# Quarter sums of w_down: made within the MLP's down product instead of beside the cross-attention

## The chip, the cores and the metric

The kernel runs on one core of one Trainium2 chip. The metric is the device time of one execution in microseconds, the median of the runs; lower is better. A profile is one further execution, taken with the hardware profiler.

## The reference

One inference step of a small streaming encoder: two layers over 1024 prompt frames and 64 sample frames (1088 columns), model width 1024, all in fp32. What matters here is the second half of every layer, and w_down above all:

```python
def cross_attn(h, mk, mv, w_q, w_o):
    q = (h @ w_q).reshape(B, L, N_MEM_HEADS, MEM_HEAD_DIM)
    s = jnp.einsum('blhd,bmhd->bhlm', q, mk).astype(jnp.float32) * (MEM_HEAD_DIM ** -0.5)
    pr = jax.nn.softmax(s, axis=-1)
    o = jnp.einsum('bhlm,bmhd->blhd', pr.astype(mv.dtype), mv).reshape(B, L, D_MODEL)
    return o @ w_o
def sq_relu_mlp(h, w_up, w_down):
    return jnp.square(jax.nn.relu(h @ w_up)) @ w_down
...
        x = x + cross_attn(rmsnorm(x, ...), mem_k[layer], mem_v[layer], p['w_mq'][layer], p['w_mo'][layer])
        x = x + sq_relu_mlp(rmsnorm(x, ...), p['w_up'][layer], p['w_down'][layer])
```

w_up is 1024 x 4096 and w_down 4096 x 1024. There are four attention heads of width 256 and 256 memory tokens.

## The kernel before, in words

**Split products.** fp32 operands go to TensorE as two fp32r parts. A split is an ACT copy that makes the high part and a DVE subtraction that makes the low part (`split`, L238 and L241; for whole weight tiles `Weights.do_split`, L185 and L186). A product takes three matmuls: low x high, high x low, high x high.

**Stages.** A memory stage and the mixer of layer 0 come first. Then each layer has its cross-attention (`cross`, for columns s = 0 of width 512 and s = 1 of width 576, each followed by `project_back` with w_mo), the up product and the down product of the MLP; layer 1 has a window attention ahead of its cross-attention.

**Cross-attention.** For each head j, `query(j)` makes two blocks of queries from w_mq tiles (`mm<-hpH,wp`), DVE scales them (L824), ACT and DVE split them into qh and ql; `scores(j)` multiplies them with k and does the softmax; `flip(j-1)` transposes the probabilities of the head before and splits them (tp); `values(j-1)` multiplies them with v. Work of one head thus stands between the steps of the next.

**Up and down products.** Both use a seven-product scheme on 2 x 2 blocks. In the down product, w_down is cut into eight groups g of 512 rows; a group has four quarters [128 x 2 x 512] (column half c, row tiles r and r + 2). `SEVEN` lists seven products m. Three of them take a quarter as it lies in w_down: (0,0), (1,1), (0,1). Four take a sum: S1 = q(1,0) + q(1,1), S3 = q(0,0) - q(1,0), S2 = S1 - q(0,0), S4 = q(0,1) - S2. The order is (0,0), (1,1), S3, S1, S2, S4, (0,1), so the products are called m0 to m6 here.

**Where the sums are made.** Before, `weights_sums` makes all four sums for a whole layer while its cross-attention runs: 32 pieces, each fetched by two DMAs that ACT issues (L966), combined by four POOL operations of 128 x 256 (L960) and stored to a scratch tensor `sums` by a DMA that ACT issues (L969). `cross` advances this generator with `next(beside)` at eight places per head. ACT works its queue in order, so a store that waits for POOL holds up what stands behind it.

**The down product's steps.** `mlp_down` has 14 steps, two halves of each m, four groups each. A step multiplies four weight tiles with four u tiles for both s. For every group of the next step it calls `W.ahead` (split a staged weight, load a later one) and `load_u` (fetch a u tile `ur` of 544 KB and split it into `uhl`). Weights land in three staging buffers `st` (`Weights.load`, L173): a load can start when the split of the weight three before it is done. Split tiles have five buffers `wd` and three `wp`, one for each group; u tiles have three buffers `ur`. All these loads stand in SP's queue. The Tile scheduler decides the order on each queue; the up product alone has a manual order on SP, POOL and PE.

```python
    for i, (m, half) in enumerate(steps):          # mlp_down
        ...
                    if after is not None and s == 0:
                        W.ahead(c + 1)
                        g = 4 * after[1] + c
                        ready[after[0], g] = load_u(us, p, after[0], g)
```

Of the kernel before, what the change touches and what calls it, by code (L numbers as in the profile page):

```python
# [7 lines left out]
F32 = mybir.dt.float32  # L8
# [5 lines left out]
D = 1024  # L14
KC = D // 128
NT1 = 512
NT2 = 576
# [16 lines left out]
S2, S3, S4, S1 = range(4)  # L34
# [12 lines left out]
def body(ctx, tc, I, O):  # L47
# [4 lines left out]
    def dram(t, offset, ap):  # L52
        return bass.AP(tensor=t.tensor, offset=t.offset + offset, ap=ap)
# [65 lines left out]
    def plan_mlp(l):  # L119
        stops.append(len(plan))  # L120
        w = I["w_down"][l]
        for m, (q, *_) in enumerate(SEVEN):
            for g in range(8):
                if isinstance(q, int):
                    src = sums[l][g][:, q]
                else:
                    src = dram(w, (4 * g + q[1]) * 128 * D + q[0] * 512, [[D, 128], [256 * D, 2], [1, 512]])
                plan.append((("down", l, m, g), "s", [(slice(0, 128), None, src)]))

    stops = []  # L130
    sums = [[scr.tile([128, 4, 2, 512], F32, name=f"sums{l}_{g}") for g in range(8)] for l in range(2)]
# [16 lines left out]
    class Weights:  # L148
        def __init__(self):
            self.loaded, self.split, self.used = 0, 0, 0  # L150
            self.stage, self.tiles = {}, {}
            self.staged, self.more = 0, None
            self.stop, self.room = stops[0], 3

        def load(self):

            if self.loaded >= self.stop or self.staged >= self.room:
                return False
            key, kind, pieces = plan[self.loaded]
            self.staged += 1  # L160
            st = wst.tile([128, 1024], F32, tag="st", name="st")
            for rows, part, src in pieces:
                if kind == "n":
                    dst = st.rearrange("p (k n) -> p k n", n=128)
                elif kind == "d":
                    dst = st.rearrange("p (k n) -> p k n", n=256)
                elif kind == "s":
                    dst = st.rearrange("p (k n) -> p k n", n=512)
                elif kind == "q":
                    dst = st.rearrange("p (k h n) -> p k h n", h=2, n=64)[:, :, part]  # L170
                else:
                    dst = st.rearrange("p (q k n) -> p q k n", q=2, n=128)[rows, part]
                nc.sync.dma_start(dst, src)  # L173
            self.stage[self.loaded] = st
            self.loaded += 1
            return True

        def do_split(self):
            st = self.stage.pop(self.split)
            key, kind, pieces = plan[self.split]  # L180
# [600 lines left out]
    def cross(l, s, norm, p, then, beside):  # L781
# [25 lines left out]
        def query(j):  # L807
# [3 lines left out]
            for c in range(2):  # L811
# [9 lines left out]
                next(beside)  # L821
# [14 lines left out]
        def scores(j):  # L836
            qh, ql = st["q", j]
            ps_of = []
            for q, bl in groups:
# [21 lines left out]
                if len(ps_of) == 1:  # L861
                    next(beside)
# [57 lines left out]
        for j in range(4):  # L920
            q = query(j)
            next(q)
            next(beside)
# [3 lines left out]
            next(beside)  # L927
            next(q, None)
            next(beside)
# [4 lines left out]
            next(beside)  # L934
            scores(j)
            load_kv(j + 1, 0, 1)
            next(beside)
# [6 lines left out]

    def weights_sums(l, p):


        keep = tc.keep_in_program_order
        tiles = {}

        def at(i):
            return sums[l][i // 4][:, :, i // 2 % 2, 256 * (i % 2):256 * (i % 2) + 256]

        for i in range(34):
            if 1 <= i <= 32:

                a = tiles[i - 1]
                for to, one, two, op in ((3, 1, 3, OP.add), (1, 0, 1, OP.subtract), (0, 3, 0, OP.subtract),
                                         (2, 2, 0, OP.subtract)):
                    keep(pool.tensor_tensor(a[:, to], a[:, one], a[:, two], op))  # L960
            if i < 32:
                a = tiles[i] = p.tile([128, 4, 256], F32, tag="quarters", name="quarters", bufs=2)
                for j in range(2):
                    rows = I["w_down"][l][256 * (i // 2) + 128 * j:256 * (i // 2) + 128 * j + 128]
                    rows = rows.rearrange("p (h n) -> p h n", h=2)[:, :, 256 * (i % 2):256 * (i % 2) + 256]
                    keep(act.dma_start(a[:, 2 * j:2 * j + 2], rows))  # L966
            yield
            if 1 <= i <= 32:
                keep(act.dma_start(at(i - 1), tiles.pop(i - 1)))  # L969
            yield  # L970
# [280 lines left out]
    def mlp_down(l, us, ready, last, p):  # L1251
# [19 lines left out]
        for i, (m, half) in enumerate(steps):  # L1271
# [4 lines left out]
            for s in range(2):  # L1276
# [4 lines left out]
                for c in range(4):  # L1281
# [369 lines left out]
    def main():  # L1651
# [36 lines left out]
        for l in range(2):  # L1688
# [12 lines left out]
            with phase(f"cross{l}") as p:  # L1701
                nexts = []
                beside = weights_sums(l, p)
                back = cross(l, 0, c1, p, lambda: nexts.append(prepared(1, G_CROSS + l)), beside)
                project_back(**back)
                back = cross(l, 1, nexts[0], p, lambda: nexts.append(prepared(0, G_MLP + l, True)), beside)
                for _ in beside:
                    pass
# [50 lines left out]
```

## Time and profile before

| | us |
|---|---|
| median of 3 runs | 2867.02 (2865.0 to 2870.07) |
| profiled execution, its own time | 2863.92 |
| its span | 2862.1 |
| PE busy | 2688.7 (94%) |
| DVE / ACT / POOL busy | 1661.9 / 1240.1 / 788.3 |
| granted TensorE clock over the span, share of full | 0.974 |
| DMA traffic | 414.22 MB, 145 GB/s mean |

Between the span and the execution's own time lie 1.8 us. PE is the busiest engine, but its share is a mean over stages: it is near 100% in the up and down products and near 80% in parts of the cross-attention. A profile of this kind is read by stage: first which stretch has idle time on PE, then what ended that idle time, then what the releasing engine had itself waited for.

### The profile page before, as it was taken

The numbers are of one execution on the slowest core, as the hardware profiler recorded it, in microseconds if no ns is written. First come the engines' busy times: TensorE is split into PE (matmuls) and PEld (weight loads), VectorE is DVE, ScalarE is ACT, GpSimd is POOL, SyncE is SP. The second block draws the span as 40 slices with busy tenths as digits, with TensorE's granted clock in tenths as the row PEclk, the third lists the DMA queues.
The fourth block names the chain that finished last, engine by engine and source line by source line (L and its number), as shares of the span: only waits on it lengthen the run. The fifth ranks groups of instructions, "written<-read, shape, count | busy, mean of one in ns | idle before, by whom it ended". The sixth has DMA issues, their size and how long they took to land. (4 is left out here: it accounts for less than half of the span.)

```text
span 2862.1 us, 47830 instructions
## 1 busy us (share of the span) xinstructions
PE 2688.7 (94%) x19048; PEld 2550.2 (89%) x19048; DVE 1661.9 (58%) x2834; ACT 1240.1 (43%) x2099; POOL 788.3 (28%) x878
## 2 busy tenths in 40 slices
PE   8999997979899999999999999879898999999998
PEld 8978996778799999999988899768798999999998
DVE  5596754556855456555457467455577454555453
ACT  5584542434444345333337347243444344443334
POOL 3200025343455652000003013343524655500000
PEclk9999998999999999999999999999999999999999
DMA  8722246564244447555331321556623444575552
GB/s 266 227 74 81 67 129 200 151 212 142 63 138 151 134 140 270 191 183 182 99 88 29 87 68 45 166 175 191 203 69 118 135 129 154 167 244 181 181 182 78
DMA packets 442276, 414.22 MB, mean 145 GB/s; under 512 B 50001, under 2 KB 398177, under 8 KB 442053
## 3 DMA queue, kind: packets, MB, share of 16 engines
q1 hardware_dynamic: 364548, 316.99, 35.5%
q10 hardware_dynamic: 68608, 67.12, 7.2%
q0 software_dynamic: 8896, 27.06, 3.0%
q8 instruction: 149, 2.44, 0.4%
q14 instruction: 75, 0.61, 0.1%
HBM read 301.84 MB, written 109.39 MB: 144 GB/s over the span
## 5 line engine op out<-in xcount | busy, mean ns | idle before, releaser
L219 PE MATMUL mm<-hpH,wp 128*128 128x288 f32 (+3 forms) x3008 | 725.5, 329 | 4.8 <-DVE wp L186 2.6
L219 PEld LDWEIGHTS mm<-hpH,wp 128*128 128x128 f32 x3008 | 517.1, 190 | 44.2 <-DVE wp L186 3.2
L219 PE MATMUL mm<-hpL,wp 128*128 128x288 f32 (+3 forms) x1504 | 473.6, 330 | 2.2 <-DVE hpL L299 2.2
L185 ACT ACTIVATE wp<-st 128x1024 fp32r<-128x1024 f32 x218 | 229.4, 1057 | 332.0 <-PE mm L219 207.9
L241 DVE TENSOR_TENSOR wp<-st,wp 128x512 fp32r<-128x512 f32 x238 | 197.7, 838 | 240.3 <-ACT wp L238 238.1
L219 PE MATMUL s<-T,wp 128*128 128x256 f32 (+1 forms) x2304 | 310.3, 292 | 24.5 <-DVE wp L241 11.5
L186 DVE TENSOR_TENSOR wp<-st,wp 128x1024 fp32r<-128x1024 f32 x218 | 270.9, 1244 | 95.5 <-ACT wp L185 94.0
L219 PEld LDWEIGHTS s<-T,wp 128*128 128x128 f32 x2304 | 299.5, 191 | 30.0 <-DVE wp L241 14.9
L219 PEld LDWEIGHTS mm<-hpL,wp 128*128 128x128 f32 x1504 | 287.8, 191 | 22.1 <-DVE hpL L299 3.3
L960 POOL TENSOR_TENSOR quarters<-quarters 128x256 f32<-128x256 f32 x256 | 220.1, 862 | 277.3 <-DMA quarters<-in_w_down_dram 259.3
L324 POOL TENSOR_TENSOR rc<-rc,mhalf 128x4 f32<-128x4 f32 (+1 forms) x21 | 22.6, 1084 | 892.5 <-DVE rc L323 892.5
L238 ACT ACTIVATE wp<-st 128x512 fp32r<-128x512 f32 x238 | 136.2, 620 | 227.8 <-POOL st L1083 203.9
L219 PE MATMUL mm<-B,wp 128*128 128x256 f32 (+1 forms) x1536 | 204.8, 289 | 0.0
L185 ACT ACTIVATE wd<-st 128x1024 fp32r<-128x1024 f32 x70 | 73.6, 1054 | 301.7 <-PE t L1292 291.0
L219 PEld LDWEIGHTS mm<-B,wp 128*128 128x128 f32 x1536 | 197.7, 189 | 0.0
L186 DVE TENSOR_TENSOR wd<-st,wd 128x1024 fp32r<-128x1024 f32 x70 | 85.6, 1225 | 151.5 <-ACT wd L185 151.5
L1290 PE MATMUL s<-uhl,wd 128*128 128x256 f32 x560 | 156.4, 281 | 3.2 <-DVE uC L1113 1.8
L1291 PE MATMUL s<-uhl,wd 128*128 128x256 f32 x560 | 157.2, 281 | 0.8 <-DVE uhl L241 0.8
L241 DVE TENSOR_TENSOR uhl<-ur,uhl 128x1088 fp32r<-128x1088 f32 x112 | 144.7, 1295 | 22.6 <-ACT uhl L238 22.5
L1292 PE MATMUL s<-uhl,wd 128*128 128x256 f32 x560 | 156.6, 280 | 0.0
L238 ACT ACTIVATE uhl<-ur 128x1088 fp32r<-128x1088 f32 x112 | 123.4, 1104 | 54.7 <-DMA ur<-u 51.8
L1135 POOL TENSOR_TENSOR ss<-uC 128x288 f32<-128x288 f32 (+1 forms) x64 | 55.3, 864 | 327.7 <-ACT uC L1134 268.5
(402 smaller groups left out, 6336.1 us busy)
## 6 DMA issues: line engine op xcount, KB each, us to landing
ur<-u SPq DMA_DIRECT2D x112, 544.0 KB, 6.1
st<-in_w_up_dram SPq DMA_DIRECT2D x68, 512.0 KB, 5.0
quarters<-in_w_down_dram ACTq DMA_DIRECT2D x128, 256.0 KB, 3.7
sums<-quarters ACTq DMA_DIRECT2D x64, 512.0 KB, 4.1
st<-sums SPq DMA_DIRECT2D x64, 512.0 KB, 5.8
st<-in_w_down_dram SPq DMA_DIRECT2D x48, 512.0 KB, 5.2
st<-in_w_mq_dram SPq DMA_DIRECT2D x32, 512.0 KB, 4.3
st<-in_w_mo_dram SPq DMA_DIRECT2D x32, 512.0 KB, 4.3
```

The lines of the kernel that those rows point to most:

```text
L185: act.activation(wt[:, 0], st, AF.Copy)
L186: dve.tensor_tensor(wt[:, 1], st, f32(wt[:, 0]), OP.subtract)
L219: m = pe.matmul(ps, a, b, start=i == 0, stop=i == len(terms) - 1)
L238: act.activation(h, src, AF.Copy)
L241: dve.tensor_tensor(l, src, f32(h), OP.subtract)
L324: pool.tensor_tensor(rc[:m, b0:b1], rc[:m, b0:b1], mhalf[:m, b0:b1], OP.pow)
L960: keep(pool.tensor_tensor(a[:, to], a[:, one], a[:, two], op))
L1135: pool.tensor_tensor(t[0], u[:, 3], u[:, 0], OP.subtract)
L1290: pe.matmul(ps, wl, uh, start=first, stop=False)
L1291: pe.matmul(ps, wh, ul, start=False, stop=False)
L1292: pe.matmul(ps, wh, uh, start=False, stop=half == 1 and g == 3 and k == 1)
```

## The change

`weights_sums` and all `next(beside)` are taken out of `cross`. The sums are made in the down product, when a weight is loaded: `Weights.load` fetches one quarter (or a kept sum) into `st`, the new `combine` fetches the other operand in two DMAs of 256 KB into a pair of small buffers, and POOL adds or subtracts in place in `st`, two operations of 128 x 512 for each operand. Three pairs of small buffers take turns: `sx` in the down phase's own pool, and the norm's `rb` and `ss`/`sq`. S1 of the even groups is made during m1 and kept in `sums`; S1 of the odd groups during m3; S2 of the even groups is kept during m4. Stores of kept sums are issued by POOL. The calls of `W.ahead` and `load_u` move from the four c of s = 0 to every second c of both s.

Counted for a layer: 36 operands fetched (72 DMAs of 256 KB), 72 POOL operations of 128 x 512, 12 kept sums of 512 KB stored, in place of 128 POOL operations of 128 x 256, 64 fetches of 256 KB and 32 stores of 512 KB. Loads and stores in a step, u tiles among them and two small fetches taken as one: 8 in m0 and m6, on average 12 in m1, m2 and m3, 14 in m4 and m5.

```diff
-                if isinstance(q, int):
-                    src = sums[l][g][:, q]
+                s1, s2, odd = sums[l][g][:, 0], sums[l][g][:, 1], g % 2
+                if q == S3:
+                    src, more, keep = quarter(0, 0), [(OP.subtract, quarter(1, 0))], None
+                elif q == S1:
+                    src, more, keep = (quarter(1, 0), [(OP.add, quarter(1, 1))], s1) if odd else (s1, [], None)
+                elif q == S2:
+                    src, more, keep = s1, [(OP.subtract, quarter(0, 0))], None if odd else s2
+                elif q == S4:
+                    src, keep = quarter(0, 1), None
+                    more = [(OP.add, quarter(0, 0)), (OP.subtract, s1)] if odd else [(OP.subtract, s2)]
                 else:
...
+                    if q == (1, 1) and not odd:
+                        more, keep = [(None, quarter(1, 0))], s1
...
+        def combine(self, st, more, keep):
+
+            for op, src in more:
+
+                tag = ("sx", "rb", "ss")[self.turn % 3]
+                self.turn += 1
+                both = []
+                for i in range(2):
...
+                    both.append(t[:, :512])
+                    nc.sync.dma_start(both[i], src[:, i])
+                for i, t in enumerate(both):
+                    part = st[:, 512 * i:512 * i + 512]
+                    if op is None:
+                        pool.tensor_tensor(t, part, t, OP.add)
+                        pool.dma_start(keep[:, i], t)
+                    else:
+                        pool.tensor_tensor(part, part, t, op)
+            if more and more[0][0] is not None and keep is not None:
+                pool.dma_start(keep, st.rearrange("p (k n) -> p k n", n=512))
...
-    def weights_sums(l, p):
...
-                    if after is not None and s == 0:
-                        W.ahead(c + 1)
-                        g = 4 * after[1] + c
+                    if after is not None and c % 2 == 0:
+                        W.ahead(2 * s + c // 2 + 1)
+                        g = 4 * after[1] + 2 * s + c // 2
                         ready[after[0], g] = load_u(us, p, after[0], g)
```

**ACT's queue in the cross-attention.** The third head of s = 0 in layer 0, before; `quarters` are the pieces of w_down, `sums` the scratch tensor, `tp` the flipped probabilities, `hpH` the high part of the attention's output:

```order
L969 DMA sums_2_86<-quarters 512x1x256
L185 ACTIVATE wp<-st 128x1024
L238 ACTIVATE qh<-q_4751 128x512
L969 DMA sums_2_86<-quarters 512x1x256
L966 DMA quarters<-in_w_down_dram 128x2x256 x2
L238 ACTIVATE v_4756<-kvst 128x512
L238 ACTIVATE tp<-t 128x512 x2
L966 DMA quarters<-in_w_down_dram 128x2x256 x2
L185 ACTIVATE wp<-st 128x1024
L969 DMA sums_3_87<-quarters 512x1x256
L238 ACTIVATE qh<-q_4814 128x512
```

The same place in the changed kernel:

```order
L227 ACTIVATE wp<-st 128x1024
L280 ACTIVATE qh<-q_4653 128x512
L280 ACTIVATE tp<-t 128x512 x2
L227 ACTIVATE wp<-st 128x1024
L280 ACTIVATE qh<-q_4707 128x512
L280 ACTIVATE hpH<-mm 128x512 x2
```

The fetches and stores are gone from between the splits; no split of the cross-attention stands behind POOL's sums any more.

**PE's queue there.** The second head of s = 0 in layer 0, before: `mm<-hpH,wp` ends the second query block, `s<-k` are scores of this head, `mm<-tp,v` the values of the head before:

```order
L219 MATMUL mm<-hpH,wp 128x512 x8
L219 MATMUL s<-k_4272,ql 128x256
L219 MATMUL s<-k_4272,qh 128x256
L219 MATMUL s<-k_4272,ql 128x256
L219 MATMUL s<-k_4272,qh 128x256
L219 MATMUL mm<-tp,v_4179 128x512 x12
L219 MATMUL s<-k_4272,ql 128x256
L219 MATMUL s<-k_4272,qh 128x256 x3
```

The same place in the changed kernel:

```order
L261 MATMUL mm<-hpH,wp 128x512 x8
L261 MATMUL mm<-tp,v_4179 128x512 x12
L261 MATMUL s<-k_4254,ql 128x256
L261 MATMUL s<-k_4254,qh 128x256
L261 MATMUL s<-k_4254,ql 128x256 x2
L261 MATMUL s<-k_4254,qh 128x256 x3
```

All twelve values now stand ahead of all scores, between the second query block and the first matmul that needs its split.

**SP's queue in the down product.** The loads of S4's weights (m5) of layer 0, before (`sums` holds the finished sum, `ur<-u` are the u tiles):

```order
L173 DMA st<-sums_3_87 128x1024
L974 DMA ur<-u_3_6480 128x1088
L173 DMA st<-sums_4_88 128x1024
L974 DMA ur<-u_4_6481 128x1088
L173 DMA st<-sums_5_89 128x1024
L974 DMA ur<-u_5_6482 128x1088
```

The same weights in the changed kernel (`sx` are the small buffers, each row a fetch of 256 KB):

```order
L188 DMA st<-in_w_down_dram 128x2x512
L981 DMA ur<-u_3_6224 128x1088
L188 DMA st<-in_w_down_dram 128x2x512
L209 DMA sx<-in_w_down_dram 128x512 x2
L188 DMA st<-in_w_down_dram 128x2x512
L209 DMA sx<-sums_5_89 128x512 x2
L188 DMA st<-in_w_down_dram 128x2x512
L209 DMA sx_13306<-sums_6_90 128x512
L209 DMA sx_13308<-sums_6_90 128x512
L209 DMA sx<-in_w_down_dram 128x512 x2
L209 DMA sx<-sums_7_91 128x512 x2
L981 DMA ur<-u_4_6225 128x1088
```

The u tiles of the next half step now stand behind fetches that wait until POOL has emptied a small buffer.

## Rows read from the trace of the kernel before

**Rows 1.** Busy time by stretch, us: PE, PEld, DVE, ACT, POOL, granted clock, DMA share, GB/s

```profile
420.00:700.00 280.00, 234.32 (x1312) 204.59 (x1311) 147.67 (x251) 101.75 (x212) 123.80 (x151) 0.93 0.59 182
1090.00:1425.00 335.00, 331.92 (x2629) 330.56 (x2628) 181.21 (x205) 125.63 (x128) 7.25 (x8) 0.99 0.55 186
1815.00:2090.00 275.00, 230.25 (x1285) 200.74 (x1284) 143.08 (x244) 97.71 (x208) 125.08 (x153) 0.94 0.60 186
2490.00:2822.00 332.00, 329.62 (x2619) 328.80 (x2619) 175.24 (x197) 123.33 (x126) 7.20 (x8) 1.00 0.52 182
```

**Rows 2.** PE's waits, 400 to 760: us in total, times, longest

```profile
PE s L219 <- DVE ql L241: 18.4, 6, 5.0
PE mm L219 <- ACT tp L238: 10.7, 4, 3.9
PE t L334 <- POOL rc L324: 2.5, 1, 2.5
```

**Rows 3.** The tile quarters: times in ns min/median/max, then who waited for it

```profile
L960 POOL TENSOR_TENSOR quarters<-quarters x256: 712/738/2819, 417.0 to 2085.4; 128x256 f32<-128x256 f32 x128
L966 ACTq DMA_DIRECT2D quarters<-in_w_down_dram x128: 547/630/1431, 411.9 to 2072.8; - x128
...
  ACT qh L238: 68.9, 15
```

**Rows 4.** Timeline within the third head of s = 0 in layer 0

```profile
472.00 4.47 PE L219 MATMUL mm<-tp,v 128*128 128x512 f32 x11 [0.34 <-DVE tp L241]
472.46 0.68 DVE L824 SCALAR_TENSOR_TENSOR q<-mm,rb 128x512 f32<-128x512 f32 x1
...
477.67 0.63 ACT L238 ACTIVATE qh<-q 128x512 fp32r<-128x512 f32 x1 [4.10 <-POOL quarters L960]
...
478.33 0.72 DVE L241 TENSOR_TENSOR ql<-q,qh 128x512 fp32r<-128x512 f32 x1 [3.51 <-ACT qh L238]
...
479.11 0.39 PE L219 MATMUL s<-k,ql 128*128 128x256 f32 x1 [2.64 <-DVE ql L241]
```

**Rows 5.** Slices of 20 us in the cross-attention, layer 0 (columns as in rows 1)

```profile
440.00:460.00 20.00, 12.13 (x54) 9.96 (x53) 9.35 (x16) 6.31 (x15) 9.86 (x12) 0.83 0.63 197
...
540.00:560.00 20.00, 20.00 (x90) 16.55 (x89) 11.60 (x15) 8.01 (x11) 3.03 (x4) 1.00 0.53 154
```

**Rows 6.** Timeline of ACT over one step of the down product, layer 0

```profile
1246.24 1.06 ACT L185 ACTIVATE wd<-st 128x1024 fp32r<-128x1024 f32 x1 [14.07 <-PE t L1292]
...
1254.33 1.06 ACT L185 ACTIVATE wp<-st 128x1024 fp32r<-128x1024 f32 x1 [2.12 <-DMA st<-sums]
1255.66 1.11 ACT L238 ACTIVATE uhl<-ur 128x1088 fp32r<-128x1088 f32 x1 [0.26 <-DMA ur<-u]
1270.16 1.06 ACT L185 ACTIVATE wd<-st 128x1024 fp32r<-128x1024 f32 x1 [13.38 <-PE t L1292]
```

**Rows 7.** POOL and DVE on st in the up product: ns min/median/max

```profile
L241 DVE TENSOR_TENSOR wp<-st,wp x238: 671/691/1772, 723.6 to 2487.8; 128x512 fp32r<-128x512 f32 x119
...
L1082 POOL TENSOR_TENSOR st<-st x34: 1262/1289/2282, 726.1 to 2480.3; 128x512 f32<-128x512 f32 x34
```

**Rows 8.** DVE's splits by line: total us, mean ns, then idle time before

```profile
L241 DVE TENSOR_TENSOR wp<-st,wp 128x512 fp32r<-128x512 f32 x238 | 197.7, 838 | 240.3 <-ACT wp L238 238.1
...
L241 DVE TENSOR_TENSOR uhl<-ur,uhl 128x1088 fp32r<-128x1088 f32 x112 | 144.7, 1295 | 22.6 <-ACT uhl L238 22.5
...
L186 DVE TENSOR_TENSOR wd<-st,wd 128x1024 fp32r<-128x1024 f32 x70 | 85.6, 1225 | 151.5 <-ACT wd L185 151.5
```

**Rows 9.** DMA issues: KB each, median us from issue to landing

```profile
ur<-u SPq DMA_DIRECT2D x112, 544.0 KB, 6.1
...
st<-sums SPq DMA_DIRECT2D x64, 512.0 KB, 5.8
```

**Rows 10.** Stretches with dense DMA (columns as in rows 1)

```profile
1105.00:1110.00 5.00, 5.00 (x36) 5.00 (x35) 2.94 (x4) 2.71 (x3) 0.00 (x0) 0.76 1.00 335
0.00:100.00 100.00, 87.38 (x664) 83.67 (x665) 56.54 (x94) 60.38 (x95) 31.09 (x58) 0.97 0.81 253
```

More of the change, by code (lines that the diff above doesn't have):

```diff
@@ L33 @@
 U11, U21, U22, T1, T2, T3, T4, U12 = range(8)
-S2, S3, S4, S1 = range(4)
+S1, S2, S3, S4 = range(4)
 SEVEN = [
@@ L123, in plan_mlp, with quarter @@
             for g in range(8):
-                if isinstance(q, int):
-                    src = sums[l][g][:, q]
-                else:
-                    src = dram(w, (4 * g + q[1]) * 128 * D + q[0] * 512, [[D, 128], [256 * D, 2], [1, 512]])
-                plan.append((("down", l, m, g), "s", [(slice(0, 128), None, src)]))
+                def quarter(c, r):
+                    return dram(w, (4 * g + r) * 128 * D + c * 512, [[D, 128], [256 * D, 2], [1, 512]])
+                s1, s2, odd = sums[l][g][:, 0], sums[l][g][:, 1], g % 2
[8 more added lines that the diff above has]
+                    more = [(OP.add, quarter(0, 0)), (OP.subtract, s1)] if odd else [(OP.subtract, s2)]
+                else:
+                    src, more, keep = quarter(*q), [], None
+                    if q == (1, 1) and not odd:
+                        more, keep = [(None, quarter(1, 0))], s1
+                plan.append((("down", l, m, g), "s", [(slice(0, 128), None, src)], more, keep))
     stops = []
-    sums = [[scr.tile([128, 4, 2, 512], F32, name=f"sums{l}_{g}") for g in range(8)] for l in range(2)]
+    sums = [[scr.tile([128, 2, 2, 512], F32, name=f"sums{l}_{g}") for g in range(8)] for l in range(2)]
     plan_dense(I["w_in_even"][0], IN_ORDER, ("in", 0))
@@ L158, in load @@
                 return False
-            key, kind, pieces = plan[self.loaded]
+            key, kind, pieces = plan[self.loaded][:3]
             self.staged += 1
@@ L173, in load @@
                 nc.sync.dma_start(dst, src)
+            if kind == "s":
+                self.combine(st, *plan[self.loaded][3:])
             self.stage[self.loaded] = st
@@ L176, in load @@
             return True
+        def combine(self, st, more, keep):
[4 more added lines that the diff above has]
+                for i in range(2):
+                    if tag == "sx":
+                        t = self.more.tile([128, 512], F32, tag=f"sx{i}", name=f"sx{i}", bufs=1)
+                    else:
+                        t = nrm.tile([128, NT2], F32, tag=tag if tag == "rb" else ("ss", "sq")[i], name="sx",
+                                     bufs=2 if tag == "rb" else 1)
+                    both.append(t[:, :512])
[5 more added lines that the diff above has]
+                        pool.dma_start(keep[:, i], t)
+                    else:
+                        pool.tensor_tensor(part, part, t, op)
+            if more and more[0][0] is not None and keep is not None:
+                pool.dma_start(keep, st.rearrange("p (k n) -> p k n", n=512))
         def do_split(self):
             st = self.stage.pop(self.split)
-            key, kind, pieces = plan[self.split]
+            key, kind = plan[self.split][:2]
             if kind == "s" and key[3] < 5:
@@ L778, in project_back, with cross @@
                 then(n)
-    def cross(l, s, norm, p, then, beside):
+    def cross(l, s, norm, p, then):
         n = WIDTH[s]
@@ L941, in cross @@
         return dict(s=s, key=("mo", l, s), pair=o, order=[range(6), range(6, 8)], spare=4 - 2 * s)
-    def weights_sums(l, p):
[L948 to L970, printed above, removed]
     def fetch_u(us, p, m, g):
```

16 lines of the change are left out of this document (3 added, 13 removed).

## The prediction

> **What bounds the kernel now.** I read the stretches first, then PE's waits in the worst of them, then what the releasing engine had waited for. In the down product PE works 331.9 of 335 us and 329.6 of 332 us [rows 1]: there it is the bound, and everything else is hidden. In the two cross-attentions it works 234.3 of 280 us and 230.3 of 275 us, at a granted clock of 0.93 and 0.94 of full [rows 1]. So 45.7 and 44.8 us of idle PE, 90.5 us together, lie in a fifth of the span.
>
> Of layer 0's idle time, 18.4 us ends with ql and 10.7 us with tp, both halves of splits; 2.5 us is a wait for the norm's factors, which the change does not touch [rows 2]. ACT makes the high part of each split, and ACT itself waited 68.9 us, in 15 places, for the pieces of w_down before a qh alone [rows 3]. The reader is to see the mechanism in one head: DVE has its scaled queries at 472.46 + 0.68 = 473.1, yet qh starts at 477.67, after 4.10 us in which ACT waited for POOL's sum; ql follows at 478.33, and PE starts 2.64 us late [rows 4]. PE, meanwhile, had 4.47 us of values to do from 472.00 [rows 4]. Without the hold the split takes 0.68 + 0.63 + 0.72 = 2.0 us [rows 4], less than the values.
>
> The clock shows the second price: 0.83 in the slice where PE worked 12.13 of 20 us, 1.00 in one without idle time [rows 5]. [...]
>
> **Part 1, idle time in the cross-attention: -68 us.** The change removes from ACT's queue 128 fetches of 0.63 us (81 us of issuing) and the 64 stores that wait for POOL, and from POOL 256 operations of 0.74 us [rows 3]. In the changed order no split stands behind them, and the twelve values stand ahead of all scores, so from the second head on 4.5 us of values cover a 2.0 us chain. What stays of the 90.5 us: some 6 us for the norm's factors (2.5 us is the larger of two waits in each layer [rows 2]), and heads without cover. The first head of a cross-attention has no values ahead of its scores, the last has no query block behind its softmax. I put 2 us, the length of the chain in [rows 4], on each of these eight places: 16 us. 90.5 - 6 - 16 = 68. If no head kept a wait it would be 84; if half of the waits only changed their cause, 34.
>
> **Part 2, clock: -20 us.** Work that took 234.3 us at 0.93 would take 217.9 at full clock, 16.4 us less; 230.3 at 0.94 gives 13.8 [rows 1]. That is 30 us for idle time of 90; with a quarter of the idle time left I count two thirds, 20. The ends are 0 (the clock falls as often) and 30.
>
> **Part 3, the down product: +6 us.** It takes over 36 operands a layer, fetched in 72 DMAs, 72 POOL operations and 12 stores.
>
> *Cover.* A step starts at 1246.24, the next at 1270.16: 23.9 us. ACT's last split of it ends at 1255.66 + 1.11 = 1256.8 and its subtraction on DVE 1.3 us later; PE does not need it before 1270 [rows 6]. About 12 us of slack stand in every step.
>
> *Chain of one weight.* The fourth weight of a step can only be loaded after the first was split, and ACT waited 2.12 us for it even before [rows 6]. Now two POOL operations of 1.29 us follow its landing, four for an odd group of S4 [rows 7]: 2.6 or 5.2 us later. From the 12 us this leaves 9 or 7.
>
> *Traffic.* In m4 and m5 a step moves 14 transfers in place of 8. The u tiles of 544 KB and weights of 512 KB [rows 9] make 14 x 0.53 = 7.4 MB in 23.9 us, 310 GB/s. A full window of this stage moved 335 GB/s [rows 10], so a step needs 22 us of DMA: it fits, with 2 us to spare. Behind the small fetches on SP's queue now stand u tiles (the order shows `ur<-u_4` behind all fetches of S4's last group); a u tile then has 6.1 us to land [rows 9] and a split behind it. With landings of 6 us I find 6 us of slack left in m5; with 9 or 10, none, and 2 to 3 us lost.
>
> *Price.* Nothing at one end. The other end is the rate of the first 100 us, 253 GB/s [rows 10]: 7.4 MB then take 29.3 us, 5.4 more than the step, in four steps a layer, and 12 transfers (6.4 MB) 25.1 us, 1.2 more, in six: 29 us a layer, 58 in all. The 335 GB/s window is of this very stage, so I stay near zero: 1.5 us for each of the four steps of m5 in the two layers, 6 us.
>
> *At nothing.* POOL: 12 x 1.29 = 15.5 us in the fullest step, 7.2 us of work in the whole stage before [rows 1, 7]. ACT and DVE get no new instruction, and their order in the down product is the same but for a few rows, so the calls spread evenly over a step change little; if they did, the 12 us cover it. SP's new issues lie in time in which it waits. Two small fetches stand among the up product's loads and wait for `rb`, whose last reader is done before the stores behind them are ready.
>
> [...]
>
> **Sum.** 2863.9 - 68 - 20 + 6 = 2781.9 beside the profiled execution. The median of the runs, 2867.0, is 3.1 above that execution, so I predict **2785 us**.
>
> **The rivals.**
> - *Loads bind the down product.* For it: 310 GB/s asked where the mean over the stage was 182 to 186 [rows 1], in-order issue on SP, three staging buffers. Against it: 335 GB/s in a window of the stage. Price 58 in place of 6: 2837.
> - *The waits change their cause.* Softmax and tp become the next to end last, the norm of the other half competes on ACT, and half of parts 1 and 2 stays: 44 us less gained, 2829. Against it: `project_back` runs at full PE on the same engines [rows 5], and the twelve values stand in the order.
> [...]
> - *Slower: the sums come to stand on the path.* SP's queue waits for POOL to empty a small buffer, the load behind it starts late, its sum ends late, and ACT, in order, holds the next step's splits. If a step has no slack left, every sum costs its two POOL operations, 2.6 us: 72 sums are 186 us, 2785 - 6 + 186 = 2965. It decides against the change from 88 / 72 = 1.2 us a sum. Against it: the 12 us of slack.
> - *The even spread does nothing:* by the order this is likely, and it is part of the forecast.
>
> **How the numbers follow.** The forecast, 2760 to 2810, has 0.64, the port's 2786 lies inside it with 0.06 of its own; loads that bind 0.11; waits that change their cause 0.11; slower 0.05; a larger gain than 2750 (parts 1 and 2 at 84 and 30 and the rest at 0 give 2753) 0.03. The range 2750 to 2840 holds the forecast and the first two rivals and leaves out the slower case, the larger gain and the case that both middle rivals meet, some 0.15. A difference of 0.2% is 5.7 us, about what a measurement of this kernel can tell from none. Slower by more than that is 0.05; within it 0.03, the two middle rivals together (2785 + 52 + 44 = 2881 at their full price, less at part of it); faster 0.92.
>
> **What would show it.** Right: the two cross-attention stretches 40 to 50 us shorter each, PE idle there near 10 us, the granted clock near 0.98; no `quarters` on ACT; in the down product PE above 97% and steps of 24 us, DMA share near 0.9 in m4 and m5, POOL near 100 us a layer. Wrong: steps of m4 and m5 above 26 us with PE released by wd or uhl, or cross-attention stretches still above 260 us, PE waiting for tp or for pr. If the steps of m1 to m3 grow as well, it is the staging chain, not the rate.

## The result

The changed kernel takes **2741.77 us** (median of 4 runs, 2736.79 to 2748.77); the kernel before, beside it on the same chip, 2867.89 (2865.0 to 2870.07). The ratio is 0.956, 95% interval 0.954 to 0.959: 126 us faster. The forecast was 2785, with a range from 2750 to 2840; the time lies below the range. The direction and the mechanism were right in the main; two of the three terms were too small.

The stages first, with whole stages (cut at the same matmuls in every kernel) in place of the stretches of [rows 1]. Busy time by stretch in the kernel before (stretch and its length, then us of PE, PEld, DVE, ACT, POOL, granted clock, DMA share, GB/s): the cross-attention and the down product of layer 0, then those of layer 1.

```profile
417.40:741.70 324.30, 277.54 (x1633) 247.17 (x1632) 185.38 (x303) 120.39 (x238) 133.97 (x159) 0.94 0.54 166
1097.90:1440.00 342.10, 338.31 (x2681) 336.62 (x2680) 181.27 (x211) 123.12 (x128) 4.22 (x5) 1.00 0.52 177
1816.60:2137.90 321.30, 275.47 (x1633) 246.05 (x1632) 184.60 (x303) 119.42 (x237) 131.71 (x158) 0.95 0.55 168
2498.20:2840.00 341.80, 339.15 (x2709) 338.00 (x2709) 177.43 (x206) 127.51 (x137) 4.20 (x5) 1.00 0.51 178
```

The same four stages in the changed kernel (profiled execution 2748.77 us, span 2747.0):

```profile
423.00:682.30 259.30, 257.82 (x1634) 235.37 (x1634) 171.09 (x303) 120.35 (x238) 24.11 (x32) 1.00 0.28 81
1040.80:1384.60 343.80, 338.47 (x2681) 336.56 (x2680) 203.63 (x212) 123.32 (x128) 131.37 (x93) 1.00 0.72 247
1761.90:2021.40 259.50, 258.09 (x1634) 235.90 (x1633) 171.16 (x303) 119.03 (x237) 24.59 (x32) 0.99 0.28 82
2379.30:2726.30 347.00, 342.33 (x2709) 340.69 (x2708) 205.82 (x209) 130.89 (x140) 132.35 (x93) 0.99 0.72 246
```

Read a row's length and the PE time behind it together: length less PE's busy time is PE's idle time. In the two cross-attentions it was 46.8 and 45.8 us and is 1.5 and 1.4: 89.7 us gone. PE's own time for the same matmuls fell from 277.54 to 257.82 and from 275.47 to 258.09, 37.1 us, with the granted clock back at 1.00 and 0.99 of full. The down products became 1.7 and 5.2 us longer, with 127 and 128 us of POOL and 70 and 68 GB/s more. 89.7 + 37.1 - 6.9 = 119.9; the other stages, which do the same work, are 4.9 us longer in this execution, and the spans differ by 115.1. The profiled execution is the slowest of the four.

All that is left of PE's waits [rows 2] in layer 0's cross-attention (us in total, times, longest):

```profile
PE t L360 <- DVE ss L350: 1.1, 1, 1.1
PE t L376 <- POOL rc L366: 0.3, 1, 0.3
```

The same piece of a head as in [rows 4] now, timeline of PE, DVE and ACT (start, us, then the instruction):

```profile
478.40 2.96 PE L261 MATMUL mm<-tp,v 128*128 128x512 f32 x12
...
478.60 0.69 DVE L865 SCALAR_TENSOR_TENSOR q<-mm,rb 128x512 f32<-128x512 f32 x1 [2.21 <-PE mm L261]
...
479.57 0.61 ACT L280 ACTIVATE qh<-q 128x512 fp32r<-128x512 f32 x1
...
480.84 0.68 DVE L283 TENSOR_TENSOR ql<-q,qh 128x512 fp32r<-128x512 f32 x1
...
481.20 0.28 PE L261 MATMUL s<-k,ql 128*128 128x256 f32 x1
```

ACT starts `qh` 0.3 us after `q` is done, where it stood 4.10 us behind POOL before, and PE goes from values to scores without a gap.

In layer 0's down product the two densest windows of m4 and m5, columns as in [rows 1]:

```profile
1206.00:1230.00 24.00, 24.00 (x194) 24.00 (x193) 13.61 (x14) 8.25 (x8) 13.95 (x10) 1.00 0.87 314
1230.00:1254.00 24.00, 24.00 (x194) 24.00 (x193) 14.88 (x21) 8.14 (x8) 12.09 (x10) 1.00 0.85 307
```

The forecast had 310 GB/s for such a step and 335 as what the stage can get; it moves 314 and 307, and PE works all 24 us. The stage's densest 48 us lie earlier, and they go above the 335: from 1062 to 1086 us it moves 355 GB/s and PE works 21.95 of 24 us, from 1086 to 1110 it moves 359 and PE works all of them. How the slack is used up shows in ACT's timeline a little later (compare [rows 6]):

```profile
1262.72 1.06 ACT L227 ACTIVATE wd<-st 128x1024 fp32r<-128x1024 f32 x1 [9.86 <-issue]
...
1280.88 1.07 ACT L227 ACTIVATE wd<-st 128x1024 fp32r<-128x1024 f32 x1 [4.73 <-POOL st L216]
...
1297.30 1.11 ACT L280 ACTIVATE uhl<-ur 128x1088 fp32r<-128x1088 f32 x1 [9.40 <-DMA ur<-u]
```

ACT waits 4.73 us for POOL's sums and 9.40 us for a u tile to land: both lie within the 12 us of slack, and PE has no wait from 1086 to 1326 us.

The groups of instructions that answer to [rows 7, 8] (total us, mean ns, idle time before):

```profile
L216 POOL TENSOR_TENSOR st<-st,sx 128x512 f32<-128x512 f32 x128 | 210.2, 1671 | 206.8 <-DMA st<-in_w_down_dram 122.5
...
L283 DVE TENSOR_TENSOR uhl<-ur,uhl 128x1088 fp32r<-128x1088 f32 x112 | 175.7, 1572 | 47.1 <-ACT uhl L280 47.0
...
L228 DVE TENSOR_TENSOR wd<-st,wd 128x1024 fp32r<-128x1024 f32 x70 | 95.4, 1365 | 105.9 <-ACT wd L227 105.9
```

POOL's operation of 128 x 512, counted at its median of 1.29 us [rows 7], takes 1.67 on average beside DVE's splits (in layer 0 the median is still 1.30, the longest 2.36; the up product's operations of that size take 1.31 to 1.37 on average), and DVE's splits went from 1295 to 1572 ns and from 1225 to 1365. In layer 0's down product they take 1532 and 1379, and 1296 and 1220 when the sums are left out (the run without sums, below): beside the sums and their DMAs they take 236 and 159 ns longer, and that stays inside the slack.

### The profile page after: what moved, and what is told of

It is laid out like the page before. It is cut to its first block, busy times and chain, and to the rows that moved or that the text cites. A ratio compares the mean times of both kernels' runs of the same rounds, so it can differ in the third digit from the quotient of the medians.

```text
span 2747.0 us, 47835 instructions
## 1 busy us (share of the span) xinstructions
PE 2657.7 (97%) x19048; PEld 2533.5 (92%) x19048; DVE 1683.4 (61%) x2834; ACT 1240.5 (45%) x2099; POOL 821.8 (30%) x798
## 5 line engine op out<-in xcount | busy, mean ns | idle before, releaser
L261 PEld LDWEIGHTS mm<-hpL,wp 128*128 128x128 f32 x1504 | 285.9, 190 | 22.4 <-DVE hpL L341 4.0
L216 POOL TENSOR_TENSOR st<-st,sx 128x512 f32<-128x512 f32 x128 | 210.2, 1671 | 206.8 <-DMA st<-in_w_down_dram 122.5
L283 DVE TENSOR_TENSOR uhl<-ur,uhl 128x1088 fp32r<-128x1088 f32 x112 | 175.7, 1572 | 47.1 <-ACT uhl L280 47.0
L228 DVE TENSOR_TENSOR wd<-st,wd 128x1024 fp32r<-128x1024 f32 x70 | 95.4, 1365 | 105.9 <-ACT wd L227 105.9
L1140 ACT ACTIVATE uC<-uC 128x1152 f32<-128x1152 f32 (+1 forms) x64 | 71.3, 1114 | 166.0 <-DVE uC L1120 166.0
```

The source lines that it names most:

```text
L216: pool.tensor_tensor(part, part, t, op)
L228: dve.tensor_tensor(wt[:, 1], st, f32(wt[:, 0]), OP.subtract)
L261: m = pe.matmul(ps, a, b, start=i == 0, stop=i == len(terms) - 1)
L283: dve.tensor_tensor(l, src, f32(h), OP.subtract)
L1140: act.activation(u, u, AF.Relu)
```

## The experiments

Twelve kernels, each in 4 runs (POOL issues stores: 10) beside the kernel before, which came to 2867.5, 2865.5 and 2868.0 us on the three chips used; the changed kernel was not run again beside them. Since the sum of the two cross-attention stages carries the gain, the table gives it for each profile: the two stages' lengths together, PE's idle time in them, and PE's busy time over that of the changed kernel (515.9), which is taken as what the clock costs. The three kernels of the down product at the end leave these stages as they are in the changed kernel, and there they take 517.5 to 518.4, so a difference of a microsecond or two says nothing.

| kernel | us | ratio, 95% | both stages | PE idle | clock |
|---|---|---|---|---|---|
| before | 2867.9 | 1 | 645.6 | 92.6 | +37.1 |
| changed | 2741.8 | 0.956 (0.954 to 0.959) | 518.8 | 2.9 | 0 |
| POOL issues all | 2855.1 | 0.995 (0.994 to 0.997) | 628.3 | 85.3 | +27.1 |
| POOL issues stores | 2873.8 | 1.002 (1.000 to 1.003) | 663.1 | 96.3 | +50.9 |
| SP issues all | 2849.2 | 0.994 (0.992 to 0.996) | 633.8 | 93.0 | +24.9 |
| ACT, no arithmetic | 2780.0 | 0.969 (0.967 to 0.971) | 563.0 | 35.6 | +11.5 |
| ACT, three tiles | 2798.9 | 0.977 (0.975 to 0.979) | 583.6 | 46.7 | +21.0 |
| ACT, three tiles, no arithmetic | 2767.2 | 0.964 (0.962 to 0.967) | 552.2 | 25.3 | +11.0 |
| SP, three tiles | 2808.9 | 0.980 (0.978 to 0.982) | 595.5 | 57.2 | +22.4 |
| SP, no arithmetic | 2734.8 | 0.954 (0.952 to 0.957) | 520.2 | 5.6 | -1.3 |
| changed, POOL kept busy | 2761.3 | 0.963 (0.961 to 0.965) | 529.4 | 14.3 | -0.8 |

The theories at the start. **A:** the sums' stores, in order on ACT, hold the splits behind them until POOL is done. **B:** POOL's operations slow DVE's that run beside them. **C:** the time that ACT spends issuing.

### Who issues the DMAs

**POOL issues fetches and stores**, from the kernel before:

```diff
-                    keep(act.dma_start(a[:, 2 * j:2 * j + 2], rows))
+                    keep(pool.dma_start(a[:, 2 * j:2 * j + 2], rows))
...
-                keep(act.dma_start(at(i - 1), tiles.pop(i - 1)))
+                keep(pool.dma_start(at(i - 1), tiles.pop(i - 1)))
```

> The kernel before, with the fetches and stores of the sums issued by POOL in place of ACT; POOL's operations stay beside the cross-attention. Theory A (ACT's queue is held by stores that wait for POOL): ACT is free, the two cross-attention stretches fall from 324 and 321 us to 260 to 270 each, the whole to 2745 to 2765. [...]

Measured: 2855.1, 0.995. That is far from A's range. POOL's 256 operations stay here, so B allows such a time, but the waits are not B's, slow operations on DVE. ACT issues nothing for the sums here, yet its waits are long. ACT's waits, then PE's, in layer 0's cross-attention (us, times, longest):

```profile
ACT k L238 <- DMA kvst<-kT: 30.3, 2, 26.2
ACT v L238 <- DMA kvst<-v: 28.4, 5, 11.1
```

```profile
PE mm L219 <- ACT tp L238: 29.9, 2, 19.4
```

POOL's queue carries the loads of k and v (`kvst`) and the sums `o`. Now they stand behind fetches and sums: ACT starts `k` at 476.9 us, after its 26.2, and PE's 19.4 for the `tp` behind it end at 480.1. The hold went with the DMAs.

**POOL issues only the stores** (the second pair of lines above):

> The kernel before, with only the stores moved from ACT to POOL; the 128 fetches stay on ACT. Theory A: no ACT instruction waits for POOL directly any more, but a fetch still waits until the store from its buffer has landed; about half of the gain, 2790 to 2820. Theory C (ACT's time of issuing, 192 issues of about 0.6 us, is what delays the splits): two thirds of the issues stay, so two thirds of the loss: 2820 to 2835. Theory B: no change, 2860 to 2870.

Measured: 2873.8, 1.002: slower, if anything. ACT's fetches, two tiles deep, still wait for POOL to be done with a tile (ACT's waits put down to `quarters` come to 76 us in layer 0), and POOL's stores now stand among its sums, 0.74 us each. B's range came nearest; the runs with POOL kept busy and with three tiles, below, speak against B as the main cause. Theory A in its narrow form, ACT's stores alone, fell with these two runs. The wider form, for the runs that follow: every in-order queue that carries a piece of the fetch, sum and store of a tile holds whatever part of the attention's chain is queued behind that piece.

**SP issues fetches and stores** (`nc.sync` in the same lines):

> The kernel before, with the fetches and the stores of the sums issued by SP instead of ACT: the same order, operations and bytes. SP's queue carries the loads of the dense weights, which are made ahead. Theory 'any shared queue' (an in-order queue that carries work of the chain is held wherever it is; POOL's cost 2855): 2820 to 2868, PE waiting for wp. Theory 'only what the split chain stands behind' (SP's loads have room, so neither the hold, 62 us in the cross-attentions, nor the issuing and landing, 44 us, is paid, only POOL's arithmetic, 10 to 20 us): 2752 to 2775.

Measured: 2849.2, 0.994, as the theory of any shared queue has it, but not with the wait that it named: in layer 0 PE did not wait for `wp`. Its longest wait was 19.2 us for POOL's `rc`, and `ACT hpH <- POOL o` came to 20.6. SP's loads have room, but POOL gets its quarters late, because SP waits in turn for a store to land before it fetches into that tile (93.7 us in layer 0), and `o` and `rc` stand behind POOL's waiting sums (102.7 us of waits for `quarters`). With three tiles on SP (below) POOL's timeline shows this in four rows:

```profile
575.26 3.17 POOL L960 TENSOR_TENSOR quarters<-quarters 128x256 f32<-128x256 f32 x4 [3.46 <-DMA quarters<-in_w_down_dram]
581.83 3.19 POOL L960 TENSOR_TENSOR quarters<-quarters 128x256 f32<-128x256 f32 x4 [3.40 <-DMA quarters<-in_w_down_dram]
584.97 0.46 POOL L913 TENSOR_TENSOR o<-o 128x128 f32<-128x128 f32 x1
585.45 3.48 POOL L960 TENSOR_TENSOR quarters<-quarters 128x256 f32<-128x256 f32 x4
```

`o`, 0.46 us of work, comes after 3.40 us of waiting and 3.19 of sums; ACT had written its input by 577.0 and stood 7.97 us idle before the split that needs it.

### How deep, and with what work

**No arithmetic**, on ACT (the sums are left out; fetches and stores stay):

```diff
-                    keep(pool.tensor_tensor(a[:, to], a[:, one], a[:, two], op))
+                    pass
```

> The kernel before without POOL's four operations on each piece (the sums are left out, the quarters are stored as they are); every fetch and store stays on ACT. Theory A: a store now waits for the fetch to land (3.7 us) and no more for 3.3 us of POOL; part of the hold goes, 2810 to 2845. Theory B: POOL is idle, so the whole gain comes, 2740 to 2760. Theory C: all issues stay, 2855 to 2870.

Measured: 2780.0, 0.969. Between A and B, and outside C: the arithmetic and all that waits for it is worth 88 us, and 38 stay over the changed kernel. Of ACT's waits in layer 0 these are put down to its own issuing:

```profile
ACT pr L856 <- issue: 21.2, 5, 5.1
ACT qh L238 <- issue: 18.8, 5, 4.8
ACT wp L185 <- issue: 15.8, 6, 4.6
```

**POOL kept busy:** the changed kernel with the kernel before's 256 operations of 128 x 256 put back, on a tile of their own, with no DMA and with nobody waiting for them.

```diff
+        a = p.tile([128, 4, 256], F32, tag="quarters", name="quarters", bufs=1)
...
+                    keep(pool.tensor_tensor(a[:, to], a[:, one], a[:, two], op))
```

> The changed kernel with 256 POOL additions of 128 x 256 on one scratch tile put back where the old sums stood, without any DMA; nobody reads them. Theory A: nothing waits for them, 2740 to 2755, cross-attention stretches 260 to 265. Theory B: DVE's splits slow down beside them, stretches above 290, the whole above 2800.

Measured: 2761.3, 19.5 us over the changed kernel, 6 above A's range and far below B's. The profiled spans differ by 12.9 us, 10.6 of them in the two stages. With no fetch to wait for, POOL runs ahead: 183 of the 256 operations lie within the stages, the others before them. At that rate all 256 would cost some 15 us there, an estimate. B's price is real and small. DVE's groups from 417 to 680 us (total us, mean ns, idle time before), first the changed kernel:

```profile
L865 DVE SCALAR_TENSOR_TENSOR q<-mm,rb 128x288 f32<-128x288 f32 (+1 forms) x24 | 12.8, 534 | 29.2 <-PE mm L261 29.0
L283 DVE TENSOR_TENSOR ql<-q,qh 128x288 fp32r<-128x288 f32 (+1 forms) x24 | 12.8, 531 | 2.7 <-ACT qh L280 2.6
...
L900 DVE TENSOR_SCALAR pr<-pr,sm 128x256 f32<-128x256 f32 (+1 forms) x36 | 11.3, 352 | 0.4
```

then with POOL kept busy:

```profile
L901 DVE TENSOR_SCALAR pr<-pr,sm 128x256 f32<-128x256 f32 (+1 forms) x36 | 20.5, 606 | 0.4
L283 DVE TENSOR_TENSOR ql<-q,qh 128x288 fp32r<-128x288 f32 (+1 forms) x24 | 18.9, 787 | 2.6 <-ACT qh L280 2.6
...
L866 DVE SCALAR_TENSOR_TENSOR q<-mm,rb 128x288 f32<-128x288 f32 (+1 forms) x24 | 12.8, 533 | 20.1 <-PE mm L261 19.8
```

`ql` goes from 531 to 787 ns and `pr` from 352 to 606, while `q`, which reads PSUM, stays at 534 and 533. Why the three differ no run here shows.

**Three tiles**, the store one beat later, on ACT:

```diff
-        for i in range(34):
+        for i in range(35):
...
-                a = tiles[i] = p.tile([128, 4, 256], F32, tag="quarters", name="quarters", bufs=2)
+                a = tiles[i] = p.tile([128, 4, 256], F32, tag="quarters", name="quarters", bufs=3)
...
-            if 1 <= i <= 32:
-                keep(act.dma_start(at(i - 1), tiles.pop(i - 1)))
+            if 2 <= i <= 33:
+                keep(act.dma_start(at(i - 2), tiles.pop(i - 2)))
```

> The kernel before, with a third tile `quarters`, so that the store of a set of sums stands one beat later behind POOL's arithmetic on ACT's queue. The same fetches, operations and bytes. Theory H (ACT is held by stores that wait for POOL's arithmetic; about 68 us of the 126): ACT's waits for POOL's `quarters` shrink from 69 us to under 15 in the first cross-attention, 2795 to 2815. Theory P (POOL's running beside DVE and the issuing itself are the price, wherever the waits stand): 2845 to 2868. If the store's landing, which the next fetch of the same tile waits for, takes over the hold: ACT waits for DMA instead, 2825 to 2845.

Measured: 2798.9, 0.977, in H's range: one tile more and the later store take 62.0 us from the two stages, with the same work and the same queue. (A third tile without the later store was not run.) The wait for POOL was not gone as H had it: ACT's waits put down to `quarters` still came to about 59 us in layer 0, over all that it was to do next (86 before; H's 69 is the wait before `qh` alone, and over both layers). They stand less often before what PE needs: PE's waits for `ql` and ACT's `tp`, 29.1 us before [rows 2], came to 7.5.

**Three tiles without arithmetic**, on ACT:

> The kernel before with three tiles, the store one beat later, on ACT, without POOL's arithmetic (the sums are left out): the store does not wait for its fetch's landing. With two tiles it took 2780.0. Theory 'landing' (ACT held by stores whose fetch has not landed is most of the 38 us over the changed kernel): 2745 to 2762. Theory 'issuing' (192 issues of 0.6 us ahead of splits, 58 us of ACT a layer, whatever they wait for): 2772 to 2782.

Measured: 2767.2, between the two ranges. Against the run with two tiles the stores' wait for their own fetch is worth 10.8 us of the stages; 32.0 stay over the same DMAs on SP (the next run). That is not the issuing alone: the longest idle time put down to it, 6.7 us before a `wp`, holds 1.9 us of issues and 4.8 in which ACT issued nothing. What ACT's queue waits for there the profile does not show.

**SP without arithmetic** (the "previous run" of the expectation is SP issues all):

> The previous run's kernel without POOL's arithmetic (the sums are left out): only fetches and stores on SP. With the same DMAs on ACT it took 2780.0, 38 us more than the changed kernel. Theory 'ACT's time' (issues and waits on ACT are the 38 us): 2738 to 2750. Theory 'traffic' (the DMAs' bytes beside the loads are): 2770 to 2785.

Measured: 2734.8, just under the range of 'ACT's time'. All the DMAs of the sums run, and the stages are as in the changed kernel. Layer 0's cross-attention, columns as in [rows 1]:

```profile
415.50:676.50 261.00, 257.71 (x1634) 234.94 (x1633) 170.99 (x303) 120.32 (x238) 23.77 (x32) 1.00 0.69 208
```

208 GB/s where the changed kernel moves 81: the bytes cost nothing there that can be told from the spread. What the DMAs cost on ACT was ACT's time, not the traffic.

**SP with three tiles:**

> The kernel before with three tiles, the store one beat later, and fetches and stores issued by SP: neither the split chain nor SP stands behind POOL's arithmetic for long. Theory 'only what the split chain stands behind': what is left over the changed kernel is POOL's arithmetic beside DVE, 10 to 20 us, 2750 to 2765, and at most 10 us under the run with two tiles on SP. Theory 'traffic': 2790 or more.

Measured: 2808.9, a number that fits 'traffic', which SP without arithmetic excludes. Over that run it adds, but for the third tile and the later store, only POOL's arithmetic, and that costs 75 us of the stages, not 10 to 20. Part of it is the `o` of the four rows above: `ACT hpH <- POOL o` 19.1 us in layer 0, and SP waited 100.8 us for stores to land.

So, step by step from the changed kernel to the one before, in us of the two stages: 1.4 for the bytes (SP, no arithmetic), 32.0 for having the DMAs on ACT, 31.4 for the arithmetic with three tiles (some 11 to 15 come without any wait, by POOL kept busy), 62.0 for two tiles and the earlier store in place of three and the later: 126.8. The size of a step depends on the order: without arithmetic the third tile is worth 10.8, and with two tiles the arithmetic 82.6. The price is in the two together.

### The down product

**The calls as before**, all of a step's splits in its first half, in the changed kernel:

```diff
-                    if after is not None and c % 2 == 0:
-                        W.ahead(2 * s + c // 2 + 1)
-                        g = 4 * after[1] + 2 * s + c // 2
+                    if after is not None and s == 0:
+                        W.ahead(c + 1)
+                        g = 4 * after[1] + c
```

> The changed kernel with the calls of loads and splits as before (all four of a step's splits in its first half). Theory 'the spread does nothing' (the prediction's): 2737 to 2747. Theory 'the spread is what makes the sums fit' (with the old calls a weight's loads follow each other too closely, and m4 and m5 wait for SP's queue and POOL): 2755 or more, with PE waiting for uhl or wd in the down product.

Measured: 2741.0 (0.957, 0.955 to 0.959), in the first theory's range. The even spread does nothing that can be measured.

**No sums**, with plain quarters of w_down in their place:

> The changed kernel with plain quarters of w_down in place of all sums: the sums, their fetches and their stores are left out, the products and splits are the same in number. What it gains is the whole price of the sums in the down product. By the stages of the two traces that price is 7 us (1.7 and 5.2): 2732 to 2738. If the difference of the stages is only spread from run to run: 2740 to 2745. If POOL beside DVE costs more than the stages show (as the busy POOL did in the cross-attention): 2715 to 2728.

Measured: 2739.6 (0.956, 0.954 to 0.958), between the first two ranges and far above the third. In the two stages the sums cost 4.2 us (690.8 against 686.6), in the medians 2.2, less than the spread: next to nothing more is to be gained at this place.

**No kept sums:** each S made anew from its 2, 3 or 4 quarters.

```diff
+                if q == S1:
+                    src, more, keep = quarter(1, 0), [(OP.add, quarter(1, 1))], None
...
+                elif q == S4:
+                    src, keep = quarter(0, 1), None
+                    more = [(OP.add, quarter(0, 0)), (OP.subtract, quarter(1, 0)), (OP.subtract, quarter(1, 1))]
...
```

> The changed kernel without kept sums: S1 is made of 2 quarters, S2 of 3, S4 of 4, each time anew; 56 additional fetches and 112 POOL operations a layer in place of 36 and 72, no stores of sums. A step of m5 then moves 20 transfers, 10.6 MB. Theory 'rate' (335 GB/s is the most that the down product gets): 32 us for a step of m5 in place of 24, 25.3 for one of m4, 2770 to 2795. Theory 'slack' (loads run far enough ahead to even the steps out, the mean being 14.1 transfers a step): 2742 to 2755. Theory 'chain' (every additional sum stands on the path with its POOL operations once the slack is gone): 2800 or more.

Measured: 2815.1 (0.983, 0.981 to 0.986), 73 us over the changed kernel. Four neighbouring windows of layer 0, columns as in [rows 1]:

```profile
1222.00:1246.00 24.00, 24.00 (x194) 24.00 (x193) 8.67 (x15) 2.45 (x3) 20.21 (x14) 1.00 0.74 237
1246.00:1270.00 24.00, 16.90 (x121) 16.43 (x120) 12.35 (x10) 8.15 (x8) 18.24 (x12) 0.86 0.73 236
1270.00:1294.00 24.00, 15.74 (x122) 15.51 (x120) 4.57 (x7) 2.12 (x2) 22.58 (x17) 0.90 0.79 258
1294.00:1318.00 24.00, 6.11 (x20) 4.65 (x20) 15.03 (x17) 6.28 (x6) 23.98 (x16) 0.50 0.85 281
```

In the last two POOL, the fifth engine of the row, works 22.6 and 24.0 us of 24 (from 1254 to 1278 all of 24.0), and PE 15.7 and 6.1. The rate is not the limit: 258 and 281 GB/s stand below the 314, and the 359, of the changed kernel. POOL gets through 16 or 17 operations in 24 us, 1.3 to 1.5 us each, and has no time left: a step of m5 asks for 24 here, 12 in the changed kernel. The total is where 'chain' put it. The way from POOL to PE is in SP's timeline:

```profile
1288.43 6.44 SPq L217 DMA_DIRECT2D sx<-in_w_down_dram  x6
1294.92 0.43 SPq L989 DMA_DIRECT2D ur<-u  x1
```

and in PE's waits in this down product, 38.3 us in all (us, times, longest):

```profile
PE s L1305 <- ACT uhl L288: 23.7, 4, 10.9
```

SP stands at the small fetches until POOL empties a buffer (47.8 us of waits between 1240 and 1320 us), a u tile is issued behind them, its split is late, and PE waits for that. This is the chain of the rival 'Slower', with POOL's throughput as the cause that the rival did not have. The count in a window does not draw the line by itself: with 14 operations in the first PE lost nothing, with 12 in the second 7.1 us. POOL stood idle from 1242.2 to 1251.8 us, waiting for a weight to land, and from then on worked almost without a pause.

## Why the prediction was right and wrong

- **What bounds the kernel, and the hold: right in the main.** PE's idle time in the cross-attention came mostly of ACT standing behind POOL's sums, and it went. Not all was that: without POOL's arithmetic 44.2 of the 126.8 us stayed, which the forecast had in its 81 us of issuing but gave no price of its own. The 68.9 us that it reads as ACT's waits beside layer 0's idle time [rows 3] are those of both layers; layer 0 has 35.3. The runs add that ACT was only one of the queues: issued by POOL or SP, the same work held `kvst`, `o` and `rc` instead, for 0.5 and 0.6% of gain.
- **Part 1, -68 us: the wrong step is the 22 us that were to stay**, "6 us for the norm's factors" and "2 us, the length of the chain, on each of these eight places". What stays is 1.1 + 0.3 us in layer 0 and 2.9 of idle time in both stages; 89.7 us went, 21.7 more than forecast (2.1 of that since whole stages have 92.6 us of idle time and not 90.5). The heads without values are covered by other work. PE's timeline at layer 0's first head, then at the last head of s = 0:

```profile
426.44 1.98 PE L261 MATMUL mm<-hpH,wp 128*128 128x512 f32 x8
428.25 0.28 PE L261 MATMUL s<-k,ql 128*128 128x256 f32 x1
...
428.73 0.39 PE L261 MATMUL mm<-hpH,wp 128*128 128x512 f32 x1
...
484.20 0.40 PE L261 MATMUL s<-hpH,wp 128*128 128x512 f32 x1
...
487.64 0.60 PE L911 MATMUL t<-ident,pr 128*128 128x128 f32 x4
...
490.37 0.63 PE L261 MATMUL mm<-tp,v 128*128 128x512 f32 x2
```

  The next head's queries (`mm<-hpH,wp` at 428.73) stand among the first head's scores; at the last head it is the back projection of the same half (`s<-hpH,wp`), whose first products need only the heads before: it runs from 484.20 through the wait for the softmax (`t<-ident,pr`) and for the values (`mm<-tp,v`). The two places could have been looked up in the changed order, and were priced from the length of a chain instead. The norm's wait for `rc`, 2.5 us in [rows 2], shrank to 0.3 too, though the change was said not to touch it. A free POOL is not the reason: without arithmetic on ACT, with two tiles or three, it is still 2.5 us in both layers. In the kernel before DVE comes to `rc` only at 527.1 us, behind 3.7 us of the norm's low parts (`hpL`), 4.1 us after PE's sum of squares; in the changed kernel those are done earlier, and `rc` follows the sum within 0.1 us.
- **Part 2, -20 us: mis-sized, 37.1.** Two steps failed. "With a quarter of the idle time left I count two thirds" fell with part 1. And the 30 us of the whole estimate were too few: the granted clock of a stretch did not give what its work lost. Here the work lost more (277.54 to 257.82 is 7.1%, where 0.94 gives 6%); with SP issuing all it lost less (269.22 to 257.82 is 4.2% in layer 0, where 0.93 gives 7%). Nor does the clock's price follow the idle time in proportion: 14.3 us of idle time cost none (POOL kept busy), 25.3 cost 11.0, 92.6 cost 37.1, and 93.0 in fewer, longer waits (SP issues all: 20 waits in layer 0, the longest 19.2 us, against 27 and 5.0 before) 24.9.
- **Part 3, +6 us: the size right, the place not.** 6.9 by the stages, 4.2 against the kernel without sums. Cover, chain and traffic came as worked out: 307 to 314 GB/s for 310, waits of 4.7 us for POOL. But the 6 us were 1.5 for each step of m5, and there nothing was lost: PE works without a gap from 1086 to 1326 us in layer 0 and from 2424 to 2688 in layer 1. It lost 2.0 us in each layer in the stage's second 24 us, at 355 and 344 GB/s (0.7 in layer 0 before). That the sum fits is in part luck. POOL needed 127 us a layer more and not about 93: its 72 operations took 118 us in layer 0, 1.64 each and not 1.29, and the issues of the kept sums' stores 9; the slack carried that as well.
- **At nothing: right.** The even spread is 2741.0 against 2741.8. SP's new issues and the waits for the small buffers show in SP's queue and not in PE's.
- **The rivals.** Loads that bind: no, not even with 112 sums' operations a layer for 72, where POOL's time came first. Waits that change their cause: not here, but it is what POOL's or SP's issuing did. The port, to which the chances give 2786: no run shows a port that DVE and POOL share. What the runs show in layer 0's down product is longer operations on both engines, DVE's splits at 1532 and 1379 ns for 1296 and 1220 without the sums, POOL's sums at 1.64 us on average for the 1.29 counted, and PE without a wait from 1086 to 1326 us all the same. The slower case did not come; its chain did, once POOL had no idle time left.
- **The sum.** 43 us between 2785 and 2741.8: 21.7 of part 1, 17.1 of part 2, -0.9 of part 3, -4.9 in stages that the change leaves alone, and 10.1 from setting medians beside profiled executions: the forecast added 3.1 for the kernel before, and the changed kernel's median is 7.0 below its profiled execution. Even the largest gain that the forecast priced, 2753, fell short: it kept 6 us for the norm and had 30 for the clock. Its chances do not quite add up either: the three cases that the range leaves out have 0.05, 0.03 and 0.03, which is 0.11 and not 0.15.

What stays open: how the 62.0 us for the third tile and the later store divide between the two and between ACT's and POOL's waits, what ACT's issues still wait for with three tiles and no arithmetic, and at what depth the sums beside the attention would cost only what POOL kept busy costs. Four tiles were not tried.

## What to carry to other kernels

Here background work with a fetch, an operation and a store hurt by the queues that it shared, little by its engine time and not measurably by its bytes: put it where none of its queues carries a link of a waiting chain, as POOL's in the down product, and check how many operations a step its engine has room for (here a step of 24 us carried 12 of 1.67 us and did not carry 24). If it must stay, another buffer and a store one beat later was worth half of the gain. And when idle time goes, look up in the new order what stands at the places where a wait would remain before giving each a price, and do not scale the clock's share by the idle time left: here the last 14.3 us of 92.6 cost no clock.

## What was not expected of the hardware

- DVE operations of one stage react differently to a busy POOL: +256 ns for `ql` and +254 for `pr`, nothing for `q`, which reads PSUM. POOL's own operations differ as well: 1671 ns on average for 128 x 512 in the down product, where the up product's operations of that size take 1307 to 1370.
- 127 GB/s more of DMA in the cross-attention (208 against 81), beside PE at 99% of its time, cost 1.4 us in 519, which is within what the same stages differ by from kernel to kernel.
